# Starting six pairs of MLP tiles ahead of the activation sums

## The chip, the cores and the metric

The kernel runs on one core of one Trainium2 chip. A core has a matrix engine (PE, with its weight loads shown as PEld), a vector engine (DVE), a scalar engine (ACT), a slower general engine (POOL), and a queue (SP) from which all transfers between memory and the on-chip buffers are issued in order. The metric is the device time of one execution in microseconds; lower is better. Times of whole executions are the median of three runs.

## The reference

Two layers over 1024 tokens of width 1024. Each layer is a self-attention mixer, a cross-attention to memory tokens and an MLP, each wrapped in norms:

```python
for l in range(DEPTH):                      # DEPTH = 2
    ...                                     # mixer, with its norms
    h = rms_norm(x, g[2])
    y = memory_cross_attention(h, mem, xa_wq[l], xa_wkv[l], xa_wo[l], xa_mem_norm[l])
    x = x + rms_norm(y, g[3])
    h = rms_norm(x, g[4])
    y = jnp.square(jax.nn.relu(h @ mlp_w1[l])) @ mlp_w2[l]
    x = x + rms_norm(y, g[5])
```

The change concerns `h @ mlp_w1` (1024 x 1024 by 1024 x 4096) and the norm that makes its `h`.

## The kernel before

Every matrix is held as a high and a low part (`split`: ACT writes the high part, DVE subtracts it for the low part), and a product is three matmuls per 128-row block: high by high, high by low, low by high.

`mlp_up` computes the hidden layer by a 2 x 2 block scheme with seven products in place of eight. The activation is cut into four blocks: b11 and b21 are the two halves of the width for tokens 0 to 511, b12 and b22 for tokens 512 to 1023. `xattn` delivers them through `pre_b`, one tile of 128 tokens at a time (t = 0 to 7): tokens 0 to 511 arrive split and raw (r0), tokens 512 to 1023 raw only (r1). `sums(c)` then forms t1, t2, t3, n4 from the raw blocks by DVE subtractions and splits them and b22, 256 tokens a call, two calls. The weights come in pairs of 128-column tiles (two tiles w1, w2 a pair, 16 pairs a layer, `NPAIR`). For a pair p:

- `weights(p)` loads w1 and w2 and splits w1.
- `begin(p)` makes the two products that need no sums: a11 by b11 into bank y (tag S), and a12 by b21 into a bank of tag T. Their sum, relu-squared, is c11. A product is 12 matmuls.
- `weight_sums(p)` forms and splits the weight sums (a22, s1, s3, s2, s4) into a ring of eight slots that lies in the buffers of the raw activations, so it starts only when the sums have read these.
- `rest(p)` makes the other five products, 60 matmuls: t2, t3 and n4 into y, on top of what `begin` left there, t1 and b22 into a second bank z. In between DVE and ACT take the results out into c12, c22, c21, square them, and form four more sums. Seven results a pair are stored to memory (`keep`).

Results pass through two rings of buffers that are taken strictly in turn: `uc` (two) for c11, `ua` (six) for c12, c22, c21, s1, s2, s4. A buffer that comes round again waits until its store has landed. The order of issue before is: weights and begin of pairs 0 and 1; sums(0), sums(1); then for each pair weight_sums, rest, and weights and begin of the pair two ahead (`LEAD`). The framework's scheduler turns this order into one instruction stream per engine: it takes the order as priority and moves an instruction up where an earlier one is not ready by its own model of time. At run time each stream is executed in order.

`mlp_down` follows, with its own rings: l_raw (three buffers) for the stored results, l_hi and l_lo for their splits, y0 to y2, and the tiles g, xt, yn, h of the norm. The rings of one stage are laid out in the order in which `R.open` names them, over the buffers of the stage before; a tile waits for the tiles that lay at its addresses. By that layout l_raw's first buffer lies over the last two of `ua`.

Of the kernel before, what the change touches and what calls it, by code (L numbers as in the profile page):

```python
# [12 lines left out]
F32 = mybir.dt.float32  # L13
# [3 lines left out]
AF = mybir.ActivationFunctionType  # L17
ALU = mybir.AluOpType
# [4 lines left out]
P = 128  # L23
# [45 lines left out]
class Net:  # L69
# [95 lines left out]
    def pre_b(self, h, dst, col, raw=None):  # L165

        nc = self.nc
        for c in range(2):
            ps = self.ps("T")
            for j in range(4):  # L170
                nc.tensor.transpose(ps[:, j * P:(j + 1) * P], h[:, (4 * c + j) * P:(4 * c + j + 1) * P], self.ident)
            v = ps.rearrange("p (k t) -> p k t", k=4)
            at = (slice(None), slice(4 * c, 4 * c + 4), slice(col, col + P))
            if dst is not None:
                self.split(dst[0][at], dst[1][at], v)
            if raw is not None:
                if c == 0:
                    nc.scalar.activation(raw[at], v, AF.Copy)
                else:
                    nc.vector.tensor_copy(raw[at], v)  # L180

    def post_norm(self, ys, g, t, x_src, x_dst, nat, yn=None, last=False):

# [824 lines left out]
    def mlp_up(self, l, act):  # L1008
# [4 lines left out]
        left = [[self.dr([P, 2, 512]) for _ in range(NPAIR // 2)] for _ in range(7)]  # L1013
        with ExitStack() as st:
            R = self.ring(st, "up")
            R.open(*((n + x, 1) for n in ("t2", "t1", "t3", "b22", "n4") for x in ("_h", "_l")), ("uc", 2), ("ua", 6), ("w_raw", 2))
            (hi, lo), (r0, r1) = act["split"][0], act["raw"]
            B = {"b11": (hi[:, 0:4], lo[:, 0:4]), "b21": (hi[:, 4:8], lo[:, 4:8])}
            for n in ("t1", "t2", "t3", "b22", "n4"):
                B[n] = tuple(R.tile([P, 4, 512], F32R, name=n + x) for x in ("_h", "_l"))  # L1020
            sr = {}

            def sums(c):
                cs = slice(256 * c, 256 * c + 256)
                b11, b21, b12, b22 = r0[:, 0:4, cs], r0[:, 4:8, cs], r1[:, 0:4, cs], r1[:, 4:8, cs]

                def put(n, src):
                    self.split(B[n][0][:, :, cs], B[n][1][:, :, cs], src)

                nc.vector.tensor_tensor(b11, b12, b11, ALU.subtract)  # L1030
                put("t1", b11)
                nc.vector.tensor_tensor(b11, b22, b11, ALU.subtract)
                put("t2", b11)
                nc.vector.tensor_tensor(b12, b22, b12, ALU.subtract)
                put("t3", b12)
                put("b22", b22)
                nc.vector.tensor_tensor(b21, b21, b11, ALU.subtract)
                put("n4", b21)

            pairs = [{} for _ in range(NPAIR)]  # L1040

            def weights(p):
                u = pairs[p]
                f = N_FF * l + 2 * p
                w1 = self.wp.tile([P, 1024], F32, name="w_raw", bufs=self.wraw_n)
                nc.sync.dma_start(w1, A["w1"][f])
                w2 = R.tile([P, 1024], F32, name="w_raw")
                nc.sync.dma_start(w2, A["w1"][f + 1])
                h = self.wp.tile([P, 1024], F32R, name="w_hi", bufs=self.w_n)
                o = self.wp.tile([P, 1024], F32R, name="w_lo", bufs=self.w_n)  # L1050
                self.split(h, o, w1)
                u["w"], u["raw"] = (h, o), (w1, w2)

            def weight_sums(p):
                u = pairs[p]
                if not sr:
                    sr["h"], sr["l"] = (self.actp.tile([P, 8, 512], F32R, name="s_" + x, tag="act_" + x) for x in ("hi", "lo"))
                    sr["n"] = 0
                w1, w2 = u["raw"]
                a11, a12, a21, a22 = w1[:, 0:512], w1[:, 512:1024], w2[:, 0:512], w2[:, 512:1024]  # L1060

                def put(n, src):
                    k = sr["n"] % 8
                    sr["n"] += 1
                    u[n] = (sr["h"][:, k], sr["l"][:, k])
                    self.split(*u[n], src)

                slot = sr["n"]
                put("a22", a22)
                nc.vector.tensor_tensor(a22, a21, a22, ALU.add)  # L1070
                put("s1", a22)
                nc.vector.tensor_tensor(a21, a11, a21, ALU.subtract)
                put("s3", a21)
                nc.vector.tensor_tensor(a11, a22, a11, ALU.subtract)
                put("s2", a11)
                nc.vector.tensor_tensor(a12, a12, a11, ALU.subtract)
                put("s4", a12)

            def product(ps, a, b, first):

                for k in range(4):
                    w = tuple(x[:, k * P:(k + 1) * P] for x in a)
                    for n, (i, j) in enumerate(((0, 0), (0, 1), (1, 0))):
                        nc.tensor.matmul(ps, lhsT=w[i], rhs=B[b][j][:, k], start=first and k == 0 and n == 0,  # L1084
                                         stop=k == 3 and n == 2, skip_group_check=True)

            def slot(name="ua"):
                return R.tile([P, 512], F32, name=name)

            def square(c):  # L1090
                nc.scalar.activation(c, c, AF.Relu)
                nc.scalar.activation(c, c, AF.Square)

            def keep(p, i, c):
                nc.sync.dma_start(left[i][p // 2][:, p % 2], c)  # L1095

            def begin(p):
                u = pairs[p]
                w = u["w"]
                u["y"] = y = self.ps("S")  # L1100
                product(y, [x[:, 0:512] for x in w], "b11", True)
                u["c11"] = c = slot("uc")
                nc.scalar.activation(c, y, AF.Copy)
                x = self.ps("T")
                product(x, [x_[:, 512:1024] for x_ in w], "b21", True)
                nc.vector.tensor_tensor(c, x, c, ALU.add)
                square(c)
                keep(p, 0, c)

            def rest(p):  # L1110
                u = pairs[p]
                y = u["y"]
                product(y, u["s2"], "t2", False)
                c12 = slot()
                nc.scalar.activation(c12, y, AF.Copy)
                z = self.ps("T")
                product(z, u["s1"], "t1", True)
                c22 = slot()
                nc.scalar.activation(c22, z, AF.Copy)
                product(y, u["s3"], "t3", False)  # L1120
                nc.vector.tensor_tensor(c22, y, c22, ALU.add)
                square(c22)
                keep(p, 3, c22)
                product(z, u["s4"], "b22", False)
                nc.vector.tensor_tensor(c12, z, c12, ALU.add)
                square(c12)
                product(y, u["a22"], "n4", False)
                c21 = slot()
                nc.scalar.activation(c21, y, AF.Relu)
                nc.scalar.activation(c21, c21, AF.Square)  # L1130
                keep(p, 1, c21)

                c11 = u["c11"]
                s1 = slot()
                nc.vector.tensor_tensor(s1, c12, c22, ALU.add)
                keep(p, 4, s1)
                nc.vector.tensor_tensor(c12, c11, c12, ALU.subtract)
                keep(p, 6, c12)
                s2 = slot()
                nc.vector.tensor_tensor(s2, s1, c11, ALU.subtract)  # L1140
                keep(p, 5, s2)
                s4 = slot()
                nc.vector.tensor_tensor(s4, c21, s2, ALU.subtract)
                keep(p, 2, s4)

            LEAD = 2
            for p in range(LEAD):
                weights(p)
                begin(p)
            for c in range(2):  # L1150
                sums(c)
            for p in range(NPAIR):
                weight_sums(p)
                rest(p)
                if p + LEAD < NPAIR:
                    weights(p + LEAD)
                    begin(p + LEAD)
        return left

    def mlp_down(self, l, left, x_src, x_dst, last):  # L1160
# [8 lines left out]
        out_act = []  # L1169
        with ExitStack() as st:  # L1170
            R = self.ring(st, "down")
            R.open(("l_hi", 4), ("l_lo", 4), ("dw_hi", 1), ("dw_lo", 1), *(("y%d" % k, 1) for k in range(3)), ("g", 2), ("xt", 2),
                   ("yn", 1), ("h", 2), ("l_raw", 3))
            y = [R.tile([P, 4, 512], F32, name="y%d" % k) for k in range(3)]
            slots = []
            for x in ("hi", "lo"):
# [358 lines left out]
```

## Time and profile before

| | |
|---|---|
| median of 3 runs | 2608.88 us (2603.36 to 2610.06) |
| profiled execution, time | 2603.31 us |
| its span, first to last instruction | 2601.3 us |
| mean granted TensorE clock | 0.97 of full |
| PE busy | 2421.2 us, 93% of the span |
| DVE busy | 1731.0 us, 67% |
| ACT busy | 1401.2 us, 54% |

The span is that of one execution; the share of busy time is a mean over stages of different character, so a change in one stage is read from that stage's rows. In a timeline row the columns are start, duration, engine, line, operation, and in brackets how long the engine sat idle before it and what ended the wait. Matmuls are pipelined: what one costs in a stream is the distance from start to start, not its duration.

### The profile page before, as it was taken

The numbers are of one execution on the slowest core, as the hardware profiler recorded it, in microseconds if no ns is written. First come the engines' busy times: TensorE is split into PE (matmuls) and PEld (weight loads), VectorE is DVE, ScalarE is ACT, GpSimd is POOL, SyncE is SP. The second block draws the span as 40 slices with busy tenths as digits, with TensorE's granted clock in tenths as the row PEclk, the third lists the DMA queues.
The fourth block names the chain that finished last, engine by engine and source line by source line (L and its number), as shares of the span: only waits on it lengthen the run. The fifth ranks groups of instructions, "written<-read, shape, count | busy, mean of one in ns | idle before, by whom it ended". The sixth has DMA issues, their size and how long they took to land. (4 is left out here: it accounts for less than half of the span.)

```text
span 2601.3 us, 34255 instructions
## 1 busy us (share of the span) xinstructions
PE 2421.2 (93%) x11493; PEld 1974.6 (76%) x11493; DVE 1731.0 (67%) x3242; ACT 1401.2 (54%) x2744; POOL 507.5 (20%) x839
## 2 busy tenths in 40 slices
PE   7999988899997799997999999989978999899998
PEld 6867877678876677875888888877766877678886
DVE  5699996688447755553655768874596555546656
ACT  5576636688356555552434458872565555434433
POOL 4321135444233000000000245541330000000002
PEclk9999998899999899998999999999988999999999
DMA  5225365563423243465776531123233443677665
GB/s 179 87 85 210 133 189 130 140 156 104 156 90 130 92 163 134 142 237 205 250 246 211 199 121 38 38 74 133 82 122 121 144 168 134 215 247 261 226 228 174
DMA packets 165661, 402.77 MB, mean 155 GB/s; under 512 B 20282, under 2 KB 38638, under 8 KB 165486
## 3 DMA queue, kind: packets, MB, share of 16 engines
q1 hardware_dynamic: 165486, 400.59, 46.6%
q8 instruction: 91, 1.49, 0.2%
q14 instruction: 84, 0.69, 0.1%
HBM read 283.47 MB, written 117.05 MB: 154 GB/s over the span
## 5 line engine op out<-in xcount | busy, mean ns | idle before, releaser
L125 ACT ACTIVATE l_hi<-l_raw 128x1024 fp32r<-128x1024 f32 x112 | 118.5, 1060 | 344.2 <-PE ps_T L1243 147.4
L196 POOL TENSOR_SCALAR rstd<-ssq 128x1 f32<-128x1 f32 x48 | 32.6, 679 | 1338.4 <-ACT junk L150 1337.3
L126 DVE TENSOR_TENSOR l_lo<-l_raw,l_hi 128x1024 fp32r<-128x1024 f32 x112 | 136.5, 1221 | 133.5 <-ACT l_hi L125 133.4
L1243 PE MATMUL ps_S<-w_hi,l_hi 128*128 128x512 f32 x480 | 191.6, 399 | 27.6 <-ACT l_hi L125 27.6
L136 PE MATMUL ps_S<-act_hi,w_hi 128*128 128x512 f32 x512 | 202.3, 397 | 3.1 <-DVE z_lo L126 1.8
L137 PE MATMUL ps_S<-act_lo,w_hi 128*128 128x512 f32 x512 | 201.0, 393 | 1.2 <-DVE act_lo L126 1.2
L138 PE MATMUL ps_S<-act_hi,w_lo 128*128 128x512 f32 x512 | 200.0, 392 | 0.0
L121 POOL TENSOR_TENSOR w_lo<-w_raw,w_hi 128x1024 fp32r<-128x1024 f32 x59 | 144.7, 2457 | 272.6 <-ACT w_hi L120 262.7
L1243 PE MATMUL ps_S<-w_lo,l_hi 128*128 128x512 f32 x480 | 188.8, 393 | 0.0
L1243 PE MATMUL ps_S<-w_hi,l_lo 128*128 128x512 f32 x480 | 187.7, 393 | 0.0
L125 ACT ACTIVATE s_hi<-w_raw 128x512 fp32r<-128x512 f32 x160 | 100.6, 631 | 99.2 <-PE ps_S L1084 82.5
L126 DVE TENSOR_TENSOR s_lo<-w_raw,s_hi 128x512 fp32r<-128x512 f32 x160 | 109.4, 686 | 58.4 <-ACT s_hi L125 45.3
L137 PE MATMUL ps_S<-w_lo,act_hi 128*128 128x512 f32 x320 | 127.4, 399 | 2.1 <-DVE w_lo L121 2.1
L136 PE MATMUL ps_S<-w_hi,act_hi 128*128 128x512 f32 x320 | 125.5, 402 | 3.6 <-DVE yn L194 3.1
L1243 PEld LDWEIGHTS ps_S<-w_hi,l_hi 128*128 128x128 f32 x480 | 91.5, 191 | 47.4 <-ACT l_hi L125 28.5
L138 PE MATMUL ps_S<-w_hi,act_lo 128*128 128x512 f32 x320 | 126.7, 396 | 0.0
L136 PEld LDWEIGHTS ps_S<-act_hi,w_hi 128*128 128x128 f32 x512 | 96.6, 189 | 25.3 <-DVE z_lo L126 2.7
L137 PEld LDWEIGHTS ps_S<-act_lo,w_hi 128*128 128x128 f32 x512 | 96.6, 189 | 20.7 <-DVE act_lo L126 2.0
L138 PEld LDWEIGHTS ps_S<-act_hi,w_lo 128*128 128x128 f32 x512 | 96.6, 189 | 19.6
L330 ACT ACTIVATE s<-s,nm 128x128 f32<-128x128 f32 (+7 forms) x128 | 98.7, 773 | 18.0 <-DVE nm L328 16.3
L1243 PEld LDWEIGHTS ps_S<-w_lo,l_hi 128*128 128x128 f32 x480 | 91.4, 190 | 20.4
L1243 PEld LDWEIGHTS ps_S<-w_hi,l_lo 128*128 128x128 f32 x480 | 90.7, 189 | 21.3
(367 smaller groups left out, 7200.8 us busy)
## 6 DMA issues: line engine op xcount, KB each, us to landing
l_raw<-dr SPq DMA_DIRECT2D x112, 512.0 KB, 4.5
dr<-ua SPq DMA_DIRECT2D x192, 256.0 KB, 2.4
w_raw<-w SPq DMA_DIRECT2D x64, 512.0 KB, 3.7
w_lo<-w SPq DMA_DIRECT2D x128, 256.0 KB, 4.1
w_hi<-w SPq DMA_DIRECT2D x128, 256.0 KB, 4.5
x_dram<-xt SPq DMA_DIRECT2D x40, 512.0 KB, 2.6
xt<-x_dram SPq DMA_DIRECT2D x40, 512.0 KB, 3.5
w_raw<-ev_fm SPq DMA_DIRECT2D x18, 512.0 KB, 4.1
```

What stands on the lines that cost most here:

```text
L121: (eng or nc.gpsimd).tensor_tensor(lo, raw, hi.bitcast(F32), ALU.subtract)
L125: self.nc.scalar.activation(hi, src, AF.Copy)
L126: self.nc.vector.tensor_tensor(lo, src, hi.bitcast(F32), ALU.subtract)
L136: nc.tensor.matmul(ps, lhsT=a[0], rhs=b[0], start=first, stop=False)
L137: nc.tensor.matmul(ps, lhsT=a[0], rhs=b[1], start=False, stop=False)
L138: nc.tensor.matmul(ps, lhsT=a[1], rhs=b[0], start=False, stop=last)
L196: nc.gpsimd.tensor_scalar(r, q[:, 0:1], q[:, 1:2] if n == 2 else 0.0, EPS, op0=ALU.add, op1=ALU.add)
L330: nc.scalar.activation(s[:, 0:n], s[:, 0:n], AF.Exp, bias=nm, scale=-1.0, accum_out=sm)
L1243: nc.tensor.matmul(banks[z][t], lhsT=x[i], rhs=w[j][:, e], start=start and b == 0 and e == 0 and n == 0, stop=b == NB - 1 and e == 1 and n ...
```

## The change

- `begin` and `weights` of six pairs (`NL`) are issued ahead of the sums' end, and the sums go by 128 tokens in four calls between them: begin 0, begin 1, sums(0), begin 2, sums(1), begin 3, sums(2), begin 4, begin 5, sums(3).
- For these six pairs the first product leaves its bank: ACT copies it to p1 (a `ua` buffer), which is stored to memory (`early`). `rest` starts y afresh, loads p1 into a `ua` buffer and c11 into a `uc` buffer, and DVE adds p1 to each of c12, c22 and c21 where ACT copied them before. So `rest` of such a pair takes seven `ua` buffers in turn.
- The raw weights of these pairs are loaded a second time for `weight_sums`. In the loop the begins of pairs 2 to 5 fall away: rest 0 to rest 3 follow each other with no begin between; begin 6 comes behind rest 4.
- `sums` does its steps in another order. Both raw copies of `pre_b` go to ACT; before, one of two went to DVE.
- In layer 0 the rings of `mlp_up` are laid out in the reverse order, and those of `mlp_down` with y0 to y2, g and xt ahead of l_hi and l_lo. l_raw stays last.

```diff
             if raw is not None:
-                if c == 0:
-                    nc.scalar.activation(raw[at], v, AF.Copy)
-                else:
-                    nc.vector.tensor_copy(raw[at], v)
+                nc.scalar.activation(raw[at], v, AF.Copy)
...
-            R.open(*((n + x, 1) for n in ("t2", "t1", "t3", "b22", "n4") for x in ("_h", "_l")), ("uc", 2), ("ua", 6), ("w_raw", 2))
+            order = ("n4", "b22", "t3", "t2", "t1") if l == 0 else ("t2", "t1", "t3", "b22", "n4")
+            R.open(*((n + x, 1) for n in order for x in ("_h", "_l")), ("uc", 2), ("ua", 6), ("w_raw", 2))
...
             def sums(c):
-                cs = slice(256 * c, 256 * c + 256)
+                cs = slice(P * c, P * c + P)
...
+            NL = 6
+            early = [self.dr([P, 512]) for _ in range(NL)]
...
-                w1, w2 = u["raw"]
+                w1, w2 = u["raw"] if p >= NL else (load1(p), load2(p))
...
                 u["c11"] = c = slot("uc")
-                nc.scalar.activation(c, y, AF.Copy)
+                p1 = slot() if p < NL else c
+                nc.scalar.activation(p1, y, AF.Copy)
+                if p < NL:
+                    nc.sync.dma_start(early[p], p1)
                 x = self.ps("T")
                 product(x, [x_[:, 512:1024] for x_ in w], "b21", True)
-                nc.vector.tensor_tensor(c, x, c, ALU.add)
+                nc.vector.tensor_tensor(c, x, p1, ALU.add)
...
             def rest(p):
                 u = pairs[p]
-                y = u["y"]
-                product(y, u["s2"], "t2", False)
-                c12 = slot()
-                nc.scalar.activation(c12, y, AF.Copy)
+                late = p < NL
+                if late:
+                    y, p1, c11 = self.ps("S"), slot(), slot("uc")
+                    nc.sync.dma_start(p1, early[p])
+                    nc.sync.dma_start(c11, left[0][p // 2][:, p % 2])
+                else:
+                    y, c11 = u["y"], u["c11"]
+
+                def out(src):
+                    c = slot()
+                    if late:
+                        nc.vector.tensor_tensor(c, src, p1, ALU.add)
+                    else:
+                        nc.scalar.activation(c, src, AF.Copy)
+                    return c
+
+                product(y, u["s2"], "t2", late)
+                c12 = out(y)
                 z = self.ps("T")
                 product(z, u["s1"], "t1", True)
-                c22 = slot()
-                nc.scalar.activation(c22, z, AF.Copy)
+                c22 = out(z)
...
-            for p in range(LEAD):
+            for p, c in ((0, None), (1, 0), (2, 1), (3, 2), (4, None), (5, 3)):
                 weights(p)
                 begin(p)
-            for c in range(2):
-                sums(c)
+                if c is not None:
+                    sums(c)
             for p in range(NPAIR):
                 weight_sums(p)
                 rest(p)
-                if p + LEAD < NPAIR:
+                if NL <= p + LEAD < NPAIR:
                     weights(p + LEAD)
                     begin(p + LEAD)
...
-            R.open(("l_hi", 4), ("l_lo", 4), ("dw_hi", 1), ("dw_lo", 1), *(("y%d" % k, 1) for k in range(3)), ("g", 2), ("xt", 2),
-                   ("yn", 1), ("h", 2), ("l_raw", 3))
+            fs, ys = (("l_hi", 4), ("l_lo", 4)), (("dw_hi", 1), ("dw_lo", 1), *(("y%d" % k, 1) for k in range(3)))
+            norm = ("g", 2), ("xt", 2), ("yn", 1), ("h", 2)
+            R.open(*(ys + norm[:2] + fs + norm[2:] if l == 0 else fs + ys + norm), ("l_raw", 3))
```

## Rows read from the trace of the kernel before

**Rows 1.** The page, busy time by engine.
```profile
PE 2421.2 (93%) x11493; PEld 1974.6 (76%) x11493; DVE 1731.0 (67%) x3242; ACT 1401.2 (54%) x2744; POOL 507.5 (20%) x839
```

**Rows 2.** Windows: stretch, length, busy time (count) by engine, clock, DMA share, GB/s.
```profile
825.00:865.00 40.00, 17.50 (x74) 13.56 (x72) 34.58 (x35) 21.35 (x32) 7.46 (x9) 0.72 0.14 54
875.00:1150.00 275.00, 275.00 (x1179) 219.66 (x1178) 158.78 (x237) 144.87 (x234) 0.00 (x0) 1.00 0.44 147
1922.00:1962.00 40.00, 19.09 (x76) 14.75 (x76) 38.05 (x42) 23.80 (x36) 7.50 (x8) 0.70 0.14 53
```

**Rows 3.** Timeline of PE, start of layer 0's MLP.
```profile
825.68 0.50 PE L1084 MATMUL ps_S<-act_hi,w_hi 128*128 128x512 f32 x1 [0.28 <-DVE yn L194]
...
843.60 1.94 PE L171 MATMUL ps_T<-ident,h 128*128 128x128 f32 x8 [7.45 <-DVE h L162]
...
852.17 0.39 PE L1084 MATMUL ps_T<-act_lo,w_hi 128*128 128x512 f32 x1
852.39 0.39 PE L1084 MATMUL ps_T<-act_hi,w_lo 128*128 128x512 f32 x1
866.43 0.79 PE L1084 MATMUL ps_T<-t_h,s_hi 128*128 128x512 f32 x1 [13.65 <-ACT s_hi L125]
...
872.61 0.63 PE L1084 MATMUL ps_S<-t_h,s_hi 128*128 128x512 f32 x1
873.04 0.43 PE L1084 MATMUL ps_S<-t_l,s_hi 128*128 128x512 f32 x1
```

**Rows 4.** Timeline of PE, start of layer 1's MLP.
```profile
1922.50 0.50 PE L1084 MATMUL ps_S<-act_hi,w_hi 128*128 128x512 f32 x1 [0.29 <-DVE yn L194]
...
1931.99 1.94 PE L171 MATMUL ps_T<-ident,h 128*128 128x128 f32 x8 [2.81 <-DVE h L162]
...
1940.64 1.94 PE L171 MATMUL ps_T<-ident,h 128*128 128x128 f32 x8 [6.72 <-DVE h L162]
...
1959.77 0.80 PE L1084 MATMUL ps_T<-t_h,s_hi 128*128 128x512 f32 x1 [10.57 <-ACT s_hi L125]
```

**Rows 5.** Timeline of ACT, first weight sums of both layers.
```profile
863.16 1.15 ACT L125 ACTIVATE s_hi<-w_raw 128x512 fp32r<-128x512 f32 x2 [2.35 <-DVE n_l L126]
...
1956.50 1.15 ACT L125 ACTIVATE s_hi<-w_raw 128x512 fp32r<-128x512 f32 x2 [1.29 <-DVE n_l L126]
```

**Rows 6.** Timeline of PE and DVE: a pair of layer 1 with a begin, then the last two pairs.
```profile
2209.55 0.40 PE L1084 MATMUL ps_S<-t_h,s_lo 128*128 128x512 f32 x1
...
2214.45 0.69 DVE L1137 TENSOR_TENSOR ua<-uc,ua 128x512 f32<-128x512 f32 x1
...
2251.33 0.40 PE L1084 MATMUL ps_S<-t_h,s_lo 128*128 128x512 f32 x1
...
2252.84 0.39 PE L1084 MATMUL ps_S<-n_l,s_hi 128*128 128x512 f32 x1
...
2254.54 0.69 DVE L1137 TENSOR_TENSOR ua<-uc,ua 128x512 f32<-128x512 f32 x1
...
2255.17 0.39 PE L1084 MATMUL ps_S<-n_h,s_lo 128*128 128x512 f32 x1
...
2268.93 0.39 PE L1084 MATMUL ps_S<-n_h,s_lo 128*128 128x512 f32 x1
```

**Rows 7.** DMA issues of the whole span: queue, count, size each, median us from issue to landing.
```profile
dr<-ua SPq DMA_DIRECT2D x192, 256.0 KB, 2.4
...
w_hi<-w SPq DMA_DIRECT2D x128, 256.0 KB, 4.5
...
Hb<-dr SPq DMA_DIRECT2D x8, 256.0 KB, 3.2
```

**Rows 8.** Timeline of SP and PE where mlp_down takes over, layer 0 and layer 1.
```profile
1194.55 0.33 SPq L1194 DMA_DIRECT2D l_raw<-dr  x1
...
1200.82 0.80 PE L1243 MATMUL ps_S<-w_hi,l_hi 128*128 128x512 f32 x1 [18.14 <-ACT l_hi L125]
...
2278.82 0.79 PE L1243 MATMUL ps_S<-w_hi,l_hi 128*128 128x512 f32 x1 [9.50 <-ACT l_hi L125]
```

More of the change, by code (lines that the diff above doesn't have):

```diff
@@ L1030, in sums, with load1, load2 @@
                 nc.vector.tensor_tensor(b11, b12, b11, ALU.subtract)
+                nc.vector.tensor_tensor(b12, b22, b12, ALU.subtract)
+                put("b22", b22)
+                nc.vector.tensor_tensor(b22, b22, b11, ALU.subtract)
+                put("t2", b22)
                 put("t1", b11)
-                nc.vector.tensor_tensor(b11, b22, b11, ALU.subtract)
-                put("t2", b11)
-                nc.vector.tensor_tensor(b12, b22, b12, ALU.subtract)
+                nc.vector.tensor_tensor(b21, b21, b22, ALU.subtract)
                 put("t3", b12)
-                put("b22", b22)
-                nc.vector.tensor_tensor(b21, b21, b11, ALU.subtract)
                 put("n4", b21)
             pairs = [{} for _ in range(NPAIR)]
+            NL = 6
+            early = [self.dr([P, 512]) for _ in range(NL)]
+            def load1(p):
+                w1 = self.wp.tile([P, 1024], F32, name="w_raw", bufs=self.wraw_n)
+                nc.sync.dma_start(w1, A["w1"][N_FF * l + 2 * p])
+                return w1
+            def load2(p):
+                w2 = R.tile([P, 1024], F32, name="w_raw")
+                nc.sync.dma_start(w2, A["w1"][N_FF * l + 2 * p + 1])
+                return w2
             def weights(p):
                 u = pairs[p]
[L1044 to L1048, printed above, removed]
+                w1 = load1(p)
+                if p >= NL:
+                    u["raw"] = w1, load2(p)
                 h = self.wp.tile([P, 1024], F32R, name="w_hi", bufs=self.w_n)
@@ L1051, in weights @@
                 self.split(h, o, w1)
-                u["w"], u["raw"] = (h, o), (w1, w2)
+                u["w"] = h, o
             def weight_sums(p):
@@ L1127, in rest @@
                 product(y, u["a22"], "n4", False)
-                c21 = slot()
-                nc.scalar.activation(c21, y, AF.Relu)
-                nc.scalar.activation(c21, c21, AF.Square)
+                if late:
+                    c21 = out(y)
+                    square(c21)
+                else:
+                    c21 = slot()
+                    nc.scalar.activation(c21, y, AF.Relu)
+                    nc.scalar.activation(c21, c21, AF.Square)
                 keep(p, 1, c21)
-                c11 = u["c11"]
                 s1 = slot()
```

## The prediction

> **What bounds the kernel now.** I read the page first: PE is busy 93% of the span [rows 1], so a gain must come from the stretches where PE stands. In the windows by stage, the body of `mlp_up` has PE busy all the time at full clock (2.4 GHz), with DVE busy 159 of 275 us and the DMA engines 44% [rows 2]; nothing is to be had there. The first 40 us of the stage look otherwise in both layers: PE is busy 17.5 and 19.1 us, at a mean clock of 0.72 and 0.70, while DVE is busy 34.6 and 38.1 [rows 2]. There the vector engine is the bound.
>
> The timeline of PE says what it waits for. In layer 0 the begins start at 825.68; PE then stands 7.45 us for the last token tile's `h` and 13.65 us for the first weight sums [rows 3]. Layer 1 repeats it with 2.81, 6.72 and 10.57 us [rows 4]. The weight sums start when the last n4 split has left the raw buffers [rows 5], so the chain behind PE's longest wait is: last token tile, two calls of `sums` on DVE, the splits of pair 0, its first product.
>
> What the stretch costs: in layer 0 from 825.68 to 873.04, where the matmuls are fast again, 47.4 us pass [rows 3]. Work in it: 48 matmuls of the two begins at 0.228 (the distance of 852.17 and 852.39 is 0.22, both rounded), 10.9; three sets of eight transposes, 1.94 a set at half clock [rows 3], so about 1 each, 3; 13 matmuls of `rest` from 866.43 to 872.61 at 0.233 (ten distances from 2252.84 to 2255.17 [rows 6]), 3.0. Lost: 30.4. In layer 1 from 1922.50 to 1959.77 37.3 pass [rows 4]; less 10.9 and 3 leaves 23.4. The slow start of `rest` costs the 6.6 us of 13 matmuls less 3.0, so 3.6, taken from layer 0 [rows 3]: 27.0. **57 us for both layers is all that can be won there.**
>
> **The change, part by part.**
>
> *Begins into the gap.* Pairs 2 to 5 bring 96 matmuls, 21.9 us a layer, that now run later at full clock. PE's own work from the first begin to `rest` 0 becomes 144 x 0.228 = 32.8, plus 3 of transposes: it would end at 861.5 and 1958.3, close to where `rest` 0 starts now (866.43, 1959.77 [rows 3, 4]). So the gap can take them.
>
> *The vector side of the gap.* Splitting four more weight tiles is 4 x 1.2 (twice a 512-column DVE operation of 0.69 [rows 6], less overlap), their adds 4 x 0.69; 36 small steps of the sums at 0.6 in a row replace 18 at 1.14 (+1.1); two or three raw copies leave for ACT (-1.5). Together +7 us. DVE's idle time in the window is 5.4 us in layer 0 and 1.9 in layer 1 [rows 2], and the adds need not stand before the sums (-2.8). The sums by 128 can use idle time earlier. `rest` 0 is then ready 4 to 12 us after PE's own work in layer 0 and 4 to 9 in layer 1; I take 5.5 in each, near the low end since the smaller steps let three of four calls go ahead of the last tile: **11 us of the 57 stay lost.** ACT gets 4 x 2.9 us more beside 21 busy of 40 [rows 2]: hidden; without that cover it would cost up to those 12.
>
> *`rest` of the early pairs.* Here the change puts in a wait. A late pair takes seven buffers of a ring of six, so p1 of pair p+1 takes the buffer that c12 of pair p had, and its load stands in SP's queue until the store of that c12 has landed. Behind it in SP wait the c11 load, stores of the pair and weight loads; on DVE, behind the add that needs p1, wait the next splits; PE waits for the freed bank. This closes a chain from one p1 to the next: landed p1, DVE add 0.7, t3 and b22 (24 matmuls, 23 distances of 0.233: 5.4), from the last matmul's start to the end of L1137 between 3.9 (2251.33 to 2254.54 + 0.69) and 5.6 (2209.55 to 2214.45 + 0.69, with weight sums between) [rows 6], store 2.4, load between 3.2 and 4.5 for 256 KB [rows 7]. Sum 15.6 to 18.6 us. A pair without begin is 60 matmuls, 14.0. I take 5.6, since weight sums lie between here too, and a load of 3.5: 17.6, so 3.6 a transition. Transitions 0-1, 1-2, 2-3, 3-4 have no begin to cover this; 4-5 has begin 6 (19.5 in all). 8 x 3.6 = **29 us lost**, between 13 and 37. It doesn't add to another stall: the last pair of layer 1, also without a begin between, takes 13.8 us from 2255.17 to 2268.93 for 48 matmuls, 11.2 [rows 6], so 2.6 of stalls of this kind go at the same time.
>
> The Trainium skill (DMA: Bandwidth & Descriptors, "Anatomy of one DMA") puts some 2 us of fixed cost on each transfer, most of it the receipt of the write, paid twice here because the load waits for the store. With its bandwidth on top, an estimate of 2.6 for each of the two would make a transition 2.9 and the sum 6 us better; the 2.4 of the trace's store agrees.
>
> *The rest of the edits.* Three DVE adds for two ACT copies and a wider c21: about 18 DVE operations of 0.6 in a late pair, 11 of 14 us, hidden beside PE; DVE becomes the bound from 24 a pair. Transfers: 1.25 MB more a pair (p1 out and in, c11 in, w1 again), 7.5 MB a layer, beside 44% of the DMA engines [rows 2]: hidden, but a reason for the higher end of the load. The raw copies on ACT: nothing, beside PE's matmuls.
>
> *Layout in layer 0.* Where `mlp_down` takes over, PE stands 18.14 us in layer 0 and 9.50 in layer 1; in layer 0 a load of l_raw goes out only at 1194.55 [rows 8], behind the norm's loads in SP. With g and xt over tiles that free earlier those loads can go sooner. Bounds: 8.6 gained (layer 1's wait) and 2 lost (l_hi now waits for t3, 12 matmuls later). I take 4 gained.
>
> **Sum:** -57 + 11 + 29 - 4 = -21. Against the profiled execution's 2603.31 (span 2601.3 and 2 around it) 2582; that execution stands 5.6 under the median of 2608.88, so **2588 us**.
>
> **The rivals.**
>
> *p1 is in time.* If DVE serves L1137 at once and loads land in 3.2, a transition costs 1.6: 13 in place of 29, 2572. For it: the scheduler can put t1 of the next pair into the wait, and the tail's 3.9. Against it: SP in order, and more traffic. With the layer 0 wait closed and the gap full, 2557.
>
> *The clock falls in the waits (slower than before).* PE would stand 3 to 4 us in each of eight transitions. Behind 2.81 us idle in layer 1 eight transposes took 1.94, the half-clock (1.2 GHz) price, as behind 6.72 [rows 4]; if each wait drops PE so, the 3.6 of a slow start is added: 8 x 3.6 = 29, giving 2617. It decides from 21 / 8 = 2.6 us a transition on. Against it: t1 or t2 in the middle would cut the wait in two. The Trainium skill (TensorE: Matmul & The Clock Gate, "HAM oscillation") describes this loop: a transfer awaited in each round throttles PE in each round. The rows show the fall once a stage, not yet in a loop.
>
> *No measurable change.* The vector chain takes the high ends (12 and 9 us in the gap) and the transitions 18.6 us: -57 + 21 + 37 - 4 = -3, 2606. For it: DVE is nearly full in layer 1's gap.
>
> **How the numbers follow.** Forecast 0.47 (2574 to 2603), p1 in time 0.24 (2556 to 2574), no change 0.15 (2601 to 2612), falling clock 0.14 (2612 to 2630). Less than 0.3% (8 us) can't be told from no change. Faster: 0.46 + 0.24 + 0.02 = 0.72; slower 0.14; same 0.14. The range 2560 to 2618 leaves out a part of the best and the worst case.
>
> **What would show it.** Right: PE nearly full at clock 1.00 from 826 to 861 and from 1923 to 1958, `rest` 0 some 5 us later; then four pairs of 17 to 18 us with PE waiting on a DVE add behind "p1 <- DMA", while SP waits for a store of `ua`; from pair 6 on 19.6 a pair as now. Wrong: late pairs at 14 to 15 us (p1 in time); PE durations of 0.63 in the late pairs (clock); `rest` 0 behind 872 and 1966 (vector bound); l_raw's wait in layer 0 unchanged or longer.

## The result and the profile after

The changed kernel takes 2649.72 us (median of 4 runs, 2647.74 to 2650.22) against 2609.47 for the kernel before (2603.36 to 2612.3): a ratio of 1.0166, 95% interval 1.0154 to 1.0179. It is 40 us slower where 21 us less were forecast. Its profiled execution takes 2649.61 (span 2647.4), 46 us more than the one of before.

The page first, busy time by engine; it answers [rows 1]: PE's share falls from 93% to 92% with the same 11493 matmuls.

```profile
PE 2443.1 (92%) x11493; PEld 1987.7 (75%) x11493; DVE 1737.3 (66%) x3298; ACT 1398.3 (53%) x2756; POOL 512.2 (19%) x839
```

Windows of after, columns as in [rows 2]. The first two are the start of the two MLPs, where [rows 2] has PE busy 17.5 and 19.1 of 40 us; the others are the late pairs of layer 0 and layer 1, where before PE was busy all the time at clock 1.00 (layer 0 in [rows 2]; the last line below is the kernel before in layer 1).

```profile
825.00:880.00 55.00, 50.31 (x221) 41.42 (x220) 48.29 (x71) 37.09 (x66) 4.16 (x7) 0.94 0.51 177
1945.00:2000.00 55.00, 49.01 (x215) 40.25 (x214) 47.05 (x69) 35.94 (x64) 2.68 (x6) 0.94 0.51 173
...
880.00:1010.00 130.00, 105.54 (x398) 79.48 (x398) 75.03 (x116) 48.22 (x77) 0.00 (x0) 0.89 0.42 144
1985.00:2135.00 150.00, 125.77 (x475) 95.94 (x475) 87.35 (x136) 57.38 (x92) 0.00 (x0) 0.90 0.43 145
...
1985.00:2135.00 150.00, 150.00 (x643) 119.50 (x642) 86.27 (x129) 81.11 (x132) 0.00 (x0) 1.00 0.43 146
```

The gap is filled, nearly as forecast. Then the late pairs lose it again. In these two stretches PE stands 24.5 and 24.2 us, and its 873 matmuls take 231.3 us where 873 x 0.233 is 203.4: 28 us more. Some 20 of it is the clock: behind the waits some 90 matmuls follow each other at about 0.43 us, half clock (1.2 GHz). The rest lies at the edges of the waits; no_p1 below, at clock 0.99, is 9.7 over the price too. The timeline of PE shows both: a first n4 matmul of pairs 0, 1 and 2 each (881.72, 901.41, 924.94), the waits between, and one of pair 5:

```profile
881.72 0.50 PE L1093 MATMUL ps_S<-n_h,s_hi 128*128 128x512 f32 x1 [0.78 <-DVE ua L1147]
...
894.16 0.50 PE L1093 MATMUL ps_S<-t_h,s_hi 128*128 128x512 f32 x1 [2.98 <-DVE ua L1136]
...
901.41 0.40 PE L1093 MATMUL ps_S<-n_h,s_hi 128*128 128x512 f32 x1
...
916.72 0.80 PE L1093 MATMUL ps_S<-t_h,s_hi 128*128 128x512 f32 x1 [6.75 <-DVE ua L1136]
917.31 0.63 PE L1093 MATMUL ps_S<-t_l,s_hi 128*128 128x512 f32 x1
...
924.94 0.39 PE L1093 MATMUL ps_S<-n_h,s_hi 128*128 128x512 f32 x1
...
978.33 0.79 PE L1093 MATMUL ps_T<-b_h,s_hi 128*128 128x512 f32 x1 [2.77 <-DVE ua L1136]
```

L1136 is the add of p1 on DVE. What it waits for, in the timelines of DVE and SP (L1128 loads p1, L1104 stores, L1166 ends c12):

```profile
893.41 0.69 DVE L1136 TENSOR_TENSOR ua<-ps_S,ua 128x512 f32<-128x512 f32 x1 [2.89 <-DMA ua<-dr]
...
906.42 0.69 DVE L1166 TENSOR_TENSOR ua<-uc,ua 128x512 f32<-128x512 f32 x1
...
915.97 0.69 DVE L1136 TENSOR_TENSOR ua<-ps_S,ua 128x512 f32<-128x512 f32 x1 [7.06 <-DMA ua<-dr]
```

```profile
888.38 0.38 SPq L1128 DMA_DIRECT2D ua<-dr  x1
...
907.14 1.30 SPq L1104 DMA_DIRECT2D dr<-ua  x3
...
912.66 0.32 SPq L1128 DMA_DIRECT2D ua<-dr  x1
...
935.61 0.32 SPq L1128 DMA_DIRECT2D ua<-dr  x1
```

So the chain I had named is there: c12 ends at 907.11, its store goes out at 907.14, and the load of the next p1 only at 912.66. But one turn of it takes 22.6 us (893.41 to 915.97), not 17.6: 13.7 from the landed p1 to the end of c12 at 907.11 (11.7 in my sum), up to 5.5 until the next load can go out (2.4), 3.3 for the load (3.5).

To set this beside other kernels I count one **loss** for each: the time from the first begin's first matmul to the first n4 matmul of a pair, less 0.233 for each matmul and 0.5 for each four transposes that PE's instruction order has between. For example pair 0 to pair 1 of layer 0: 19.69 less 60 x 0.233 is 5.7. The losses are of the profiled executions, us, layer 0 / layer 1. The medians are of five groups of runs, in which the kernel before had 2606 to 2610; each ratio below is to before in the same group, and kernels of different groups are compared by these ratios where a few microseconds matter:

```
kernel            lost at pair 0   pair 0 to 6    pair 6 to 15   median of runs
before             30.1 / 26.1      0.3 / 0.3      4.4 / 3.7      2609
after               7.0 /  8.2     36.5 / 38.6    10.5 / 9.5      2649.7
p1_uc               7.4 /  8.2     25.3 / 22.4     4.3 / 3.7      2609.0
half_w              7.1 /  8.1     34.6 / 32.9     6.0 / 9.1      2639.6
nl4                16.0 / 15.6     20.6 / 20.6     4.4 / 3.6      2620.7
nl0                25.8 / 24.3      0.4 / 9.2      4.4 / 16.0     2624.6
sums128            22.9 / 25.7      0.4 / 0.5      5.9 / 3.8      2604.6
sums128_layout     26.7 / 24.0      0.6 / 0.6      5.9 / 3.8      2605.4
uc_oldlay          11.6 /  8.6     23.5 / 21.8     4.3 / 4.1      2615.8
warm                7.0 /  7.5     23.2 / 25.2     9.5 / 9.7      2657.7
inplace             6.8 /  8.2     48.1 / 45.7     5.9 / 3.8      2659.7
uc_rawold          13.2 /  8.9     23.9 / 22.4     4.3 / 4.1      2621.8
uc_q_raw           16.0 /  8.0     32.6 / 29.9     5.8 / 3.7      2641.3
aft_q               7.3 /  8.4     42.0 / 42.4     4.3 / 9.6      2656.9
w2_ahead            6.8 /  8.3     26.8 / 21.2     5.9 / 4.2      2610.7
w2_ahead4          15.9 / 17.1     17.4 / 20.4     4.4 / 3.9      2624.5
w2_ahead4_old      18.5 / 15.9     18.3 / 20.3     4.4 / 3.7      2627.8
no_p1               6.9 /  8.2     15.0 / 15.1    10.5 / 9.9      2607.4
```

After against before: -41.0 at pair 0, +74.5 from pair 0 to 6, +11.9 from there to the last pair. At the takeover by the down product PE stands 2.4 us less ([rows 8] has 18.14 and 9.50):

```profile
1216.57 0.80 PE L1273 MATMUL ps_S<-w_hi,l_hi 128*128 128x512 f32 x1 [16.19 <-ACT l_hi L125]
...
2324.81 0.79 PE L1273 MATMUL ps_S<-w_hi,l_hi 128*128 128x512 f32 x1 [9.03 <-ACT l_hi L125]
```

From the first of these to the last product of layer 1's cross-attention 725.1 us pass, 720.6 before: +4.5. The sum is +47.5, against 46 between the spans; the rest is work that stands on another side of these marks.

By transition, layer 0 loses 5.7, 9.5, 4.5, 2.2, 11.0 and 3.6, layer 1 5.7, 9.2, 6.3, 3.1, 11.5 and 2.8.

### The profile page after: what moved, and what is told of

It reads as the page before. It is cut to its first block, busy times and chain, and to the rows that moved or that the text cites. A ratio compares the mean times of both kernels' runs of the same rounds, so it can differ in the third digit from the quotient of the medians.

```text
span 2647.4 us, 34392 instructions
## 1 busy us (share of the span) xinstructions
PE 2443.1 (92%) x11493; PEld 1987.7 (75%) x11493; DVE 1737.3 (66%) x3298; ACT 1398.3 (53%) x2756; POOL 512.2 (19%) x839
## 5 line engine op out<-in xcount | busy, mean ns | idle before, releaser
L1093 PE MATMUL ps_S<-t_h,s_hi 128*128 128x512 f32 x256 | 107.9, 422 | 27.6 <-DVE ua L1136 19.1
L1093 PE MATMUL ps_S<-t_h,s_lo 128*128 128x512 f32 x256 | 106.4, 416 | 7.8 <-DVE s_lo L126 7.8
L327 ACT ACTIVATE s<-s,nm 128x128 f32<-128x128 f32 (+7 forms) x128 | 98.8, 774 | 17.5 <-DVE nm L325 16.5
```

Of the source, the lines that this page charges most:

```text
L327: nc.scalar.activation(s[:, 0:n], s[:, 0:n], AF.Exp, bias=nm, scale=-1.0, accum_out=sm)
```

## The experiments

Theory A: p1 takes a buffer of the ring `ua` that c12's store holds, and this wait costs the time. Theory B: the second load of w1 and the other new transfers fill the queues. Theory C: the other edits cost. Four kernels tell them apart.

**p1_uc: p1 of five of the six late pairs from another ring.** The last late pair's p1 stays in `ua`.

```
-  y, p1, c11 = self.ps("S"), slot(), slot("uc")
+  y, p1, c11 = self.ps("S"), slot("uc" if p < NL - 1 else "ua"), slot("uc")
```

> Five of the six late pairs take the buffer for p1 from the ring uc, not ua. A late pair then takes six of the six ua buffers, and p1 of the next pair waits only for the n4 add of this one, not for the store of its c12. In the trace of after, the six transitions from pair 0 to pair 6 lose 36.5 us in layer 0 and 38.6 in layer 1 (distance of the first n4 matmuls less the work between). Theory A (the chain through c12's buffer makes the wait): the transitions lose 4 us or less each instead of 5 to 11, the half-clock matmuls behind the waits go too, and the time falls by 45 to 60 us to 2590 to 2605. Theory B (the second load of w1 and the other new transfers fill the queue, and weights and p1 land late whatever buffer they take): the traffic is the same, so 2635 to 2650.

2608.96 us, 1.0015 of before (1.0004 to 1.0027): 40.8 us less than after, nearly all that the change lost, and a little above the 2590 to 2605 of theory A. The transitions lose 47.7 in place of 75.1, so 27.4 of the gain is theirs. Another 12.0 comes from the pairs behind them, which are as quick as before; no p1 is loaded there, and what makes these pairs quick or slow follows under nl0. Theory A holds for the 27.4, though the transitions did not come down to 4 each. One thing was not held apart: with the new buffer the build also puts b22 ahead of t3 in the first late pairs on PE, where after has t3 first, so the 27.4 is of buffer and order together. That the store holds the load is seen in SP's rows of after above. The windows of this kernel, columns as above:

```profile
880.00:1010.00 130.00, 113.25 (x448) 85.39 (x447) 80.90 (x125) 55.06 (x88) 0.00 (x0) 0.96 0.49 161
1985.00:2135.00 150.00, 134.20 (x545) 102.40 (x544) 92.64 (x143) 66.17 (x107) 0.00 (x0) 0.98 0.48 157
```

PE stands 32.6 us (48.7 in after), and its 993 matmuls take 247.5 where 231.4 is the full-clock price: 16 for 28, of which the matmuls at half clock are 8 for 20. The traffic is the same and its rate higher (161 GB/s for 144), which speaks against B.

**half_w: half the late weight loads.** A late pair loads 1 MB of weights for its weight sums: w1 a second time, and w2, which in these pairs is loaded only here. half_w loads 512 of the 1024 columns of each and uses them twice, so it leaves half of these weights out of the result.

```
-  w1, w2 = u["raw"] if p >= NL else (load1(p), load2(p))
+  w1, w2 = u["raw"] if p >= NL else (load1(p, 512), load2(p, 512))
```

> The weight sums of the six late pairs load only the first 512 columns of their two weight tiles and use them for both halves (so half of these weights is left out of the result): the transfers of the reload fall from 1 MB to 0.5 MB a pair, and nothing else changes. Theory A (ring chain): p1 still waits for c12's store, so at most 10 us are won: 2638 to 2650. Theory B (traffic): most of the 75 us goes: 2590 to 2615.

2639.58, 10 less than after. The transitions lose 7.6 less, and layer 0 has 4.5 less behind them, since it is built with the loop of before. Theory B has a small part.

**nl4: four early pairs** (`NL = 4`, the last call of the sums after begin 3).

> Four early pairs instead of six. Theory A: only transitions 0-1 and 1-2 are without a begin between; they lost 15.2 and 14.9 us in after, the covered ones 2-3 and 3-4 little, and two begins less in the gap give back 11 us a layer of the 18 to 23 won: 2609 + 30 - 20 = 2619, between 2612 and 2626. Theory B: the loss goes with the number of pairs that load w1 again, 4/6 of 75 us: 2609 + 50 - 20 = 2639.

2620.73 (1.0064, 1.0047 to 1.008), the sum that A gives, but in part by luck: A put the loss at 0-1 and 1-2. The transitions lose 7.3, 1.0, 9.1, 3.2 and 7.6, 0.9, 8.8, 3.2. The dearest is the one with the fewest matmuls between, 48, here 2-3, in after 4-5.

**nl0: no early pairs** (`NL = 0`, two begins, then four calls of the sums).

> No early pairs at all: the sums by 128 in their new order, the raw copies on ACT and the layout of layer 0 alone, with two begins ahead of the sums as before. Theories A and B, by which the late pairs cost the time: within 5 us of before, 2604 to 2614. Theory C (the other edits or the new order of instructions that they bring cost a part): 2615 or more. The later pairs (6 to 15) lost 2.7 us a layer more in after than in before; if that comes from the new order of the sums it is seen here too.

2624.59 (1.008): a miss for A and B, and at first sight theory C. But layer 0 has won 4.3 at pair 0 and loses nothing behind it. Only layer 1 loses, 1.4 a pair more than before in its steady loop, and there the program has another order of products on PE. The loops of before, of nl0's layer 1 and of after (1, 2, 3, b, n are the products of t1, t2, t3, b22, n4, 12 matmuls where no number follows, B those of a begin):

```
before, a pair:        B*2 B*2 1*5 B*10 B*4 n B*6 1*7 2 b
                       B*2 B*2 1*6 3 B*10 B*10 1*3 n 1*3 2 b 3   (two pairs make a turn)
nl0, layer 1, a pair:  B*2 B*2 1 3 B*10 B*10 n b 2

after, two pairs:      B*4 1 B*7 n B*13 b*10 2*2 b*2 2*10
                       B*4 1*9 B*9 3 B*11 1*3 n b 2 3
```

The order is made when the program is built, from all of its instructions, and small edits tip it. The table bears this out: in all its kernels the layers that have the order of before, to a matmul, lose 3.6 to 6.0 behind pair 6, those that have the order of after 9.1 to 10.5 (after, warm and no_p1 in both layers, half_w and aft_q in layer 1).

**sums128 and sums128_layout: the order held.** The kernel before with the sums by 128 alone, and with the layout of layer 0 too; both have PE's loop of before in both layers.

> The kernel before with the sums by 128 tokens in their new order alone: no early pairs, raw copies and layout as before. In the instruction order of this kernel PE's steady loop is the one of before in both layers (in the run without early pairs layer 1 had another loop, 1.4 us longer a pair, and lost 19 us there). If the new loop was what made that run slow, and not the sums, this gives before's time or less: the first n4 of layer 0 came 4.3 us of lost time earlier there, of layer 1 1.8, so 2600 to 2608. If the small sums or their extra instructions cost time themselves: 2612 or more.

> As the run before it, with the layout of layer 0 in its new form as well. My step said 4 us won at the takeover by the down product. The traces of all kernels with the new layout show 1 to 4 us less wait there, but from the takeover to the first begin of layer 1 they take 726 to 730 us where before takes 721.7. By the step: 2 to 4 us less than the run before it. By the traces: 2 to 5 us more, with the wait shorter and the stretch behind it longer.

2604.55 (0.9982, 0.9972 to 0.9993) and 2605.41 (0.999, 0.998 to 1.0). So C falls as far as the sums and the layout go; what nl0 lost in layer 1 goes with the loop. The layout wins 1.1 us of wait (16.77 for 17.84 in layer 0) and nothing to be seen in the time; the stretch behind the takeover, to the same mark as above, takes 720.5 us in both, so my reading that the layout costs there was wrong too.

**uc_oldlay: p1_uc with the old layout.**

> p1 of five late pairs from the ring uc, and the layout of layer 0 as before. If the layout costs more behind the takeover than it wins there: 2602 to 2608 (3 to 6 us less than with p1 in uc alone, 2609). If it wins 4 as my step said: 2613.

2615.78 (1.0032, 1.002 to 1.0043): 7 more than p1_uc by the medians, some 4 by the ratios. The traces don't show it. The two profiled executions take the same (2612.33 and 2612.97); the wait at the takeover is 17.68 for 14.87, but the stretch behind it is 3.3 shorter. Before pair 0 of layer 0 4.2 more are lost, yet the first begin is 3.8 earlier. So the new layout is worth between nothing and the 4 I gave it, and the runs don't settle which.

**warm: 12 matmuls more in each late pair.**

```
   product(z, u["s1"], "t1", True)
+  if late:
+      product(self.ps("T"), u["s1"], "t1", True)
```

> The changed kernel with 12 more matmuls in each late pair: the product for t1 a second time into a PSUM tile that nothing reads, 144 matmuls or 33.6 us in all at full clock. In after the twelve transitions lose 75 us: 47 of it PE stands, 28 are matmuls at half clock behind the waits. If the waits are for p1 and the clock falls because PE stands in them, the extra matmuls run inside the waits and cost less than they take, and some of the 28 comes back: 2625 to 2650. If PE's work is what sets the late pairs, or the clock would not fall anyway, all of the 33 us is added: 2670 to 2685.

2657.73: 33.6 us of work cost 8.0, so PE's work doesn't set the late pairs. Two things pay for the other 25.6. PE stands less, 32.1 us in place of 48.7 in the two stretches. And the clock falls less: the granted clock rises from 0.89 and 0.90 to 0.95 and 0.94, and the 988 matmuls take 17.7 over the full-clock price in place of 28.

```profile
880.00:1010.00 130.00, 114.39 (x455) 87.85 (x454) 71.19 (x110) 46.83 (x73) 0.00 (x0) 0.95 0.43 147
1985.00:2135.00 150.00, 133.51 (x533) 102.97 (x532) 86.75 (x135) 56.79 (x91) 0.00 (x0) 0.94 0.46 151
```

**inplace: c21 over p1, six buffers a pair** (`c21 = out(y, p1)`).

> The changed kernel with c21 of a late pair written over its p1, so that a late pair takes six buffers of the ring of six. The load of the next p1 now waits for s4 to have read c21 (two vector operations behind c12's end) and no longer for the store of c12. Its instruction order has PE's steady loop of before. Theory A: each transition is shorter by the store (2.4 to 4.3 us) less two vector operations (1.4), ten of them 10 to 29 us, and the steady loop gives 12 back: 2610 to 2628. If the wait were not on the ring: 12 us for the loop alone, 2638.

2659.66, a miss: slower than after. The transitions lose 18.7 more, and the pairs behind them, in the loop of before, 10 less. SP's timeline shows why:

```profile
892.83 0.32 SPq L1128 DMA_DIRECT2D ua<-dr  x1
...
911.69 0.93 SPq L1129 DMA_DIRECT2D uc<-dr  x1
912.71 0.93 SPq L1104 DMA_DIRECT2D dr<-ua  x1
916.60 0.32 SPq L1128 DMA_DIRECT2D ua<-dr  x1
```

The loads of p1 for pairs 1 and 2 are 23.8 us apart (892.83 and 916.60) as in after (24.3), and the first comes 4.5 later. c21 is ready for its store only after two more steps on ACT, so the buffer is still given back by a store, of another tile. That the store is in the way whichever tile is stored fits A; my count of what frees the buffer was wrong.

**uc_rawold, uc_q_raw, aft_q: raw copies, and another queue.** uc_rawold is p1_uc with the raw copies half on DVE; uc_q_raw (uc_rawold with one more edit) and aft_q (after with the same edit) issue the loads of p1 and c11 by GpSimd, with p1 in `uc` and in `ua`:

```
-  nc.sync.dma_start(p1, early[p])
-  nc.sync.dma_start(c11, left[0][p // 2][:, p % 2])
+  nc.gpsimd.dma_start(p1, early[p])
+  nc.gpsimd.dma_start(c11, left[0][p // 2][:, p % 2])
```

> p1 of five late pairs from the ring uc, and the raw copies half on DVE as before. In every kernel so far with all raw copies on ACT the stretch from the down product of layer 0 to the layer 1 begins took 3 to 7 us more than before; in the two with the old copies it took the same. If the copies, or the order that comes with them, do this: 2602 to 2606. If not: 2609 to 2612, since DVE takes two or three copies back in each gap.

> As the run before it, with the loads of p1 and c11 issued by GpSimd, whose queue is empty here, instead of behind the stores and weight loads in SP's. With p1 in uc the twelve transitions still lost 48 us. If a part of that is SP's order (a wait of 3.4 us for p1 in transition 1-2 of layer 0, 1.5 to 2.4 in 4-5): 5 to 12 us less than the run before it. If what is left are the dependences inside a pair without a begin and the late weight loads: the same within 3 us.

> The changed kernel, with its buffers as they are, and the loads of p1 and c11 issued by GpSimd. PE's steady loop is that of before in layer 0 and that of after in layer 1. Theory A (the wait for c12's store is bound to the buffer, whatever queue the load stands in): 6 us for the loop and up to 10 for what waits behind the load in SP: 2632 to 2645. If the order in SP's queue and not the buffer makes p1 late: 2605 to 2618.

2621.83, 2641.29 and 2656.86: three misses. With the raw copies back on DVE the kernel takes 13 us more than p1_uc by the medians, 8 by the ratios (1.0045 for 1.0015); the first n4 of layer 0 comes 11.1 later (895.18 for 884.07). In this pair of kernels, which differ in the copies and in the order built from them, ACT's copies are not worth nothing, as I had it. Another queue makes uc_rawold worse by 19. Against after it wins nothing: the ratio is 1.0179 (1.0151 to 1.0207) for 1.0166, with 9.3 more lost in the transitions and 6.2 less behind them in layer 0, by the loop. GpSimd's queue isn't free: in its timeline (uc_q_raw) p1's load (L1131) stands behind c11's (L1132), which waits for the last reader of the former c11.

```profile
898.65 0.54 POOL L1132 DMA_DIRECT2D uc<-dr  x1 [15.34 <-DVE ua L1172]
899.25 0.54 POOL L1131 DMA_DIRECT2D uc<-dr  x1
```

In uc_q_raw its loads also land later. From the DMA issues of uc_q_raw (count, KB, median us from issue to landing):

```profile
uc<-dr POOLq DMA_DIRECT2D x22, 256.0 KB, 4.6
```

The same row of uc_rawold:

```profile
uc<-dr SPq DMA_DIRECT2D x22, 256.0 KB, 3.5
```

In aft_q it is so for c11 alone; after has 3.2 from SP for both:

```profile
ua<-dr POOLq DMA_DIRECT2D x12, 256.0 KB, 3.0
uc<-dr POOLq DMA_DIRECT2D x12, 256.0 KB, 5.2
```

The Trainium skill (DMA: Bandwidth & Descriptors, "Issuing engine by pattern") calls the Sync queue generally the faster for plain loads; here the landings agree in uc_q_raw and for c11 in aft_q, not for p1 in aft_q, and GpSimd's queue has an order of its own beside that. aft_q also has both loops in one kernel: layer 0, with the loop of before, loses 4.3 from pair 6 on, layer 1, with that of after, 9.6.

**w2_ahead, w2_ahead4, w2_ahead4_old: the second weight tile.** All three have p1 in `uc` as p1_uc has it. The second weight tile of the last late pair is asked for ahead of the next pair's, with six and with four early pairs, the last kernel with raw copies and layout of before:

```
-  w1, w2 = u["raw"] if p >= NL else (load1(p), load2(p))
+  w1, w2 = u["raw"] if p >= NL else (load1(p), u["w2"] if "w2" in u else load2(p))
...
+  if p + LEAD == NL:
+      pairs[p + 1]["w2"] = load2(p + 1)
```

> p1 of five late pairs from the ring uc, and the second weight tile of pair 5 asked for ahead of that of pair 6, so that it isn't left with one buffer of two. With p1 in uc alone, transition 4-5 lost 7.1 and 9.4 us and 5-6 4.8 and 3.2, with PE waiting 2.6 us for weight sums. If the late weight tile makes these two: 4 us in place of 12 in each layer, 2590 to 2598. If it is the pair without a begin or p1(5), which stays in ua: 2604 to 2612.

> The same with four early pairs. The run with four early pairs and nothing mended (2621) lost 7.3, 1.0, 9.1 and 3.2 us in its transitions. With p1 in uc and the weight tile ahead both mended: 3, 1, 2 and 2, so 2592 to 2602. If only the first is mended: 2608 to 2614.

> As the run before it, with raw copies and layout as before the change. In four runs so far the raw copies on ACT went with 3 to 6 us more behind the down product of layer 0, in a pair of runs that differed in them the other way round (2609 with, 2622 without). No theory of the late pairs speaks of them: the same as the run before it within 8 us.

2610.65 (0.9999, 0.9989 to 1.001), 2624.5 and 2627.79. The transition 4-5 still loses 7.2 and 7.0 (7.1 and 9.4 in p1_uc), with four early pairs 2-3 10.6 and 9.5: the second weight tile isn't it. w2_ahead4 misses both of its numbers and is no quicker than nl4 (1.0055 for 1.0064). With four early pairs p1's buffer gives little: the transitions lose 37.8 for 41.2, and 20 of the 37.8 stand at 2-3, where the last late pair has its p1 in `ua` still. The last two kernels, which differ in copies and layout, are 3.3 apart.

**no_p1: no load of p1 and c11.**

```
-  nc.sync.dma_start(p1, early[p])
-  nc.sync.dma_start(c11, left[0][p // 2][:, p % 2])
...
-  nc.vector.tensor_tensor(c, src, p1, ALU.add)
+  nc.vector.tensor_copy(c, src)
...
+  c11 = c22
```

> The changed kernel without the loads of p1 and c11: the late pairs copy PSUM where they added p1, and use c22 where they used c11 (p1 and c11 are left out of the result). A late pair takes six buffers and waits for no load but the weights'. PE's steady loop is that of after, 12 us longer in all. If p1's load is all that a late pair waits for: the transitions lose 10 to 20 us in all in place of 75, 2585 to 2598. If, as with p1 in uc, 48 stay because of the dependences of a pair without a begin and of the weight tiles: 2618 to 2625.

2607.39 (0.9989, 0.9978 to 1.0001), between the two expectations. The transitions lose 30.1 of 75.1, and PE's clock holds (0.99 in both stretches):

```profile
880.00:1010.00 130.00, 119.50 (x492) 91.45 (x491) 84.11 (x129) 59.39 (x94) 0.00 (x0) 0.99 0.46 155
1985.00:2135.00 150.00, 139.52 (x578) 107.70 (x577) 91.71 (x141) 67.10 (x108) 0.00 (x0) 0.99 0.44 147
```

So the two loads with all that hangs on them make 45 us, 27 of it the part that p1_uc takes away. Of the 30 that stay, the transitions 0-1 to 3-4 make 11.6 (1.9, 1.8, 0.9, 0.9 and 1.8, 1.9, 0.8, 1.6), 4-5 makes 12.3 and 5-6 6.2. Even with p1 for nothing the change, in this order, would not beat the kernel before by more than the measurement can tell. The loop of after behind pair 6 is 12 us of that; without it the time would be some 2595, an estimate.

## Why the prediction was wrong

**The gap was right.** 57 us less 11 gave 46; measured are 41.0 (23.1 and 17.9). PE is busy 50 and 49 of the first 55 us. The six pairs' products do run where PE stood.

**The step that failed is the `rest` of the early pairs**, 29 us with an upper end of 37; it measured 74.5, and no rival had that: the dearest ended at 2630. The chain named is there, and what p1_uc takes away with it, 27.4, is near the 29. That is partly luck, since the turn was mis-sized. What was wrong is that the chain was the whole price: 18 more hang on the loads of p1 and c11, and 30 stay with neither of them loaded (no_p1). By steps:

- A turn of the chain took 22.6 and not 17.6 where I followed it. The durations came from the kernel before, without this traffic: while p1 is awaited the DMA engines move 338 GB/s at 0.89 busy (window 910 to 915 of after), against 147 and 0.44 in [rows 2]. The Trainium skill's estimate that stands beside the sum, 2.6 for each of the two transfers (DMA: Bandwidth & Descriptors, "Anatomy of one DMA", where the fit is given for transfers that GpSimd issues), was further off: here 5.5 and 3.3. PE also runs a part of this turn at half clock.
- I put this wait and the falling clock down as rivals. They came together: 48.7 us of standing, and some 20 of half-clock matmuls where the rival had 29. The clock should have been a part of the forecast and not an alternative at 0.14; even that rival's 2617 lacks the stalls and the loop below. I had written that the rows show the fall once a stage, but [rows 4] has half-clock starts behind three waits in a row (2.81, 6.72 and 10.57). Against the rival I had said that t1 or t2 would cut the wait in two. PE does run them first, and then still stands 6.75 us at 916.72 and 6.42 at 2036.26, with matmuls of 0.79 behind. The Trainium skill (TensorE: Matmul & The Clock Gate, "HAM oscillation") has this loop of an awaited transfer and a throttled engine; here the trace agrees, with the clock at 0.50 to 0.70 between 910 and 920.
- I counted four transitions a layer without a begin's full cover, and 19.5 for 4-5. In PE's order begin 6's two products stand in 2-3 and 3-4; 4-5 has 48 matmuls and lost 11.0 and 11.5, the most of all.
- I let the wait run beside the stalls that a pair without a begin has anyway. no_p1 shows these alone: 11.6 us in eight transitions, 18.5 more at the end of the early pairs.

Two windows of after, columns as in [rows 2], the stretch in which p1 of pair 2 is awaited and the one in which PE starts again:

```profile
910.00:915.00 5.00, 0.00 (x0) 0.00 (x0) 0.00 (x0) 0.00 (x0) 0.00 (x0) 0.70 0.89 338
915.00:920.00 5.00, 3.28 (x8) 2.61 (x9) 1.29 (x2) 0.00 (x0) 0.00 (x0) 0.50 0.01 3
```

**A term was missing.** I took the pairs from 6 on to be as before. They lose 11.9 us more, most of it since the program's order on PE settles in another loop. aft_q, half_w and p1_uc show that the loss goes with the order and not with any one edit. The prediction puts nothing there ("from pair 6 on 19.6 a pair as now") and gives no reason for it.

**The small terms.** The layout: 4 forecast in layer 0; its wait is 2.0 shorter, and in the time it is worth between nothing (sums128_layout) and some 4 (uc_oldlay). The raw copies: nothing forecast; with them on DVE uc_rawold takes some 8 us more by the ratios. "Hidden" transfers: 7.6 us in half_w's transitions for 0.5 MB a pair, where I had used the traffic only for the higher end of one load.

**Open.** What makes the last late pair's two transitions 18.5 us in no_p1 isn't settled. PE waits there for weight sums (2.24 us for s_lo at 960.45), and the second weight tile was shown not to be it; the first one was not tried alone. Nor is it settled where the 3 to 6 us between the takeover and layer 1 come from: kernels with and without the raw copies on ACT have them. Of all kernels only sums128 is quicker than before with an interval clear of 1, by 0.18%, less than counts here.

## What to carry to other kernels

Work that is moved ahead takes away the cover of the place it came from: price that place with the work gone, its waits and PE's clock behind them added up, before counting the gap that it fills. Where a load takes its buffer from a ring that stores drain, the store's way to memory is in each turn; count the buffers that a turn takes against the ring, and find for the load a buffer that a compute step frees. And compare the built order of instructions: a loop that an edit doesn't touch can settle in another rhythm.

## What the runs showed of the hardware

Loads of 256 KB took a median of 3.5 us from SP's queue (uc_rawold) and 4.6 from GpSimd's (uc_q_raw), in kernels that differ in the queue and in the order built from it; in aft_q GpSimd's medians were 3.0 and 5.2. And the clock often fell only after PE had started again. Behind a wait of 2.98 us (894.16) and one of 2.57 (972.07) the first matmul took 0.50, and those that followed took 0.60 to 0.63, at half clock, soon after. The matmul at 978.33, with 0.79 behind 2.77 us, found the clock already low. So the first matmul behind a wait doesn't tell what the wait cost; the window after it does:

```profile
894.97 0.60 PE L1093 MATMUL ps_S<-t_h,s_hi 128*128 128x512 f32 x1
...
972.07 0.50 PE L1093 MATMUL ps_S<-t_h,s_lo 128*128 128x512 f32 x1 [2.57 <-DVE s_lo L126]
...
973.65 0.63 PE L1093 MATMUL ps_S<-t_h,s_lo 128*128 128x512 f32 x1
...
895.00:900.00 5.00, 5.00 (x16) 3.92 (x15) 1.19 (x2) 1.05 (x2) 0.00 (x0) 0.66 0.03 11
```
